# A hybrid decoder step on one core: conditioning vectors, result copies, query layout and a buffer moved together

## The chip, the cores and the metric

The kernel runs on 1 core of one Trainium2 chip. The metric is the device time of one execution of the whole program, in microseconds (us). One core has five engines with a queue of instructions each: TensorE (PE; its weight loads are shown as PEld), VectorE (DVE), ScalarE (ACT), GpSimd (POOL) and SyncE (SP), which here does nothing but issue transfers. Each engine takes its instructions in the order in which they stand in its queue, and an instruction that has to wait holds up the rest of the queue.

## The reference: what is computed

One layer of a decoder with two kinds of heads side by side, for a prompt of 1024 rows and for 8 samples of 4 rows (1056 rows in all), 1024 wide, in float32:

```python
sh1, sc1, g1, sh2, sc2, g2 = split(silu(c) @ w_ada + b_ada)      # conditioning: 9 vectors c, 6 parts of 1024
u = x * (1 + sc1) + sh1
mq, mk, mv, mo, mi, mf, nq, ck, cv, sk, sv, wk, wv, ng = split(u @ w_in)
h = mlstm(mq, mk, mv, mi, mf, mo)            # 4 heads of 128: a matrix memory in chunks
o = nsa(nq, ...)                             # 8 query heads of 64 in 2 groups: compressed, selected, window keys
x = LN(alpha * x + g1 * (concat(h, o) @ w_out))
u2 = x * (1 + sc2) + sh2
y = LN(alpha * x + g2 * (relu(u2 @ w_up) ** 2 @ w_down))
```

Returned beside y are the key and value rows of the step (ck, cv, sk, wk, sv, wv), the window cache moved on by four rows, and the states of the matrix memory. Only sh1 and sc1 (the first third of the conditioning) are needed for the input projection; g1 is needed after w_out, the rest from the feed-forward on.

## The kernel before

Rows are kept as columns: a tile is [128 features, rows]. Most products run as three products of two halves (a high and a low part, made by `split`: one ACT copy, one DVE subtraction). The order of the work:

- **Start.** `ada_part(G, c0, ...)` (L140) is one unit of the conditioning: four 512 KB pieces of w_ada (tile wada) are loaded over SP, 32 narrow products per unit are made (L147; the trace counts two instructions for each), then a copy and a transposition (L151) follow. There are 12 units: G is the third (0, 1, 2), c0 goes from 0 to 3. The four of G = 0 run here, with four wada buffers. Then come u and its split (uh, ul), the compression of the cache, and the products for v and the gates (L292).
- **Projections.** `proj` (L357) makes one 128-column tile of `u @ w_in` in three chunks of rows, 24 products each; its loop gives control back six times per chunk. `nsa_tile(mt)` (L454) projects one tile and stores it in DRAM: through a staging tile rw with three buffers into d_q (queries, tiles 16 to 19), d_k or d_ck. Tiles 14 to 19 come first, with the gate chain between them; then the attention of the samples (L785 to L891, its pool on the right side of memory and four banks of PSUM); then tiles 12 and 13, the compression for the prompt (`cmp_prompt`, L470), and the first steps of the matrix-memory heads (`run_dense(FILL)`).
- **Attention.** For each of 64 (group, block of 128 queries, head) `score_steps` (L959) makes scores, softmax and a probability tile P, of which there are NP = 4; `turn` (L1014) transposes it, `products` (L1059) multiplies with V. `attention_kv` (L919) and `attention_v` (L938) load keys and values once per group, `q_prep` (L946) loads queries once per block from d_q, all through the tag "qr", which has one buffer. Beside it run the "dense" steps: `mlstm_steps` (L540), with the eight remaining conditioning units in it (`ada_unit`, L530, wada with two buffers), and, when those are done, the output projection (`wout_steps`). A loop (L1175 to L1211) lays the three streams out by model costs: attention in all counts 196, dense DEN_TOTAL, and whichever is behind its share goes next.
- **End.** Output projection and first norm, the up projection in 16 pairs (`up_pair`, L1431: a Strassen-like scheme, weights aw with three buffers, results to d_r), the down projection (L1530) and the second norm.

Four copies of results from DRAM to DRAM are written at the head of attention (L913 to L917): o_v (1.1 MB), o_kT twice (1.1 MB each) and o_win (2.1 MB).

The text gives the order in which things are traced. The order in each engine's queue is set when the program is built, from a simulated timeline (`schedule_with_timeline_sim=True`): an instruction whose inputs are there can stand ahead of one written earlier. So the trace has the o_v copy at 94.94 us, in the middle of the projections, though it is written after them. A pool that is opened where another has been closed waits, tile by tile, until the old tiles have been read.

Of the kernel before, what the change touches and what calls it, by code (L numbers as in the profile page):

```python
# [31 lines left out]
T = 1056  # L32
# [26 lines left out]
def _body(tc, nc, top, io, dbg):  # L59
# [55 lines left out]

    d_q = mk(dr, [128, 4, T], F32, "d_q")
    d_k = mk(dr, [2, 128, T], F32, "d_k")
# [21 lines left out]

    def ada_part(G, c0, wpool, wbufs, pp, ps, ptile):  # L140

        for k in range(8):
            if k % 2 == 0:
                w = mk(wpool, [128, 2, 4, 128], F32, "wada", bufs=wbufs, name=f"wada{G}{c0}{k}")
                SP.dma_start(w, io["w_ada"][G, c0, :, k:k + 2])
            for j in range(4):
                PE.matmul(ps[32 * j:32 * j + 32, 0:128], lhsT=sil[:, k, :], rhs=w[:, k % 2, j],  # L147
                          start=(k == 0), stop=(k == 7), tile_position=(0, 32 * j))
        sb = mk(pp, [128, 128], F32, "adasb", bufs=1, name=f"adasb{G}{c0}")
        ACT.copy(sb, ps[:, 0:128])  # L150
        PE.transpose(ptile[:, 0:128], sb, ident)  # L151
        v = ptile[:, 0:128].rearrange("p (j i) -> p j i", j=4)
        DVE.tensor_tensor(out=adaT[:, 4 * G:4 * G + 4, c0], in0=v[:, :, 0:9],
                          in1=bc(badaT[:, 16 * G + c0:16 * G + 16:4], 9), op=ALU.add)

    sc1p = mk(ce, [128, 8, 9], F32, "sc1p")
# [296 lines left out]

    def nsa_tile(mt, between=None):  # L454
        def evac(ps, c, t0, n):
            rw = mk(pB, [128, 384], F32, "rw", bufs=3, name=f"rw{mt}_{c}")
            if mt >= 16:
                ACT.mul(rw[:, 0:n], ps[:, 0:n], -0.125)  # L458
                SP.dma_start(d_q[:, mt - 16, t0:t0 + n], rw[:, 0:n])
            else:  # L460
                ACT.copy(rw[:, 0:n], ps[:, 0:n])
                dst = (d_ck if mt < 14 else d_k)[mt % 2]
                SP.dma_start(dst[:, t0:t0 + n], rw[:, 0:n])
            next(between or iter(()), None)
        for _ in proj(mt, evac):
            pass

# [34 lines left out]

    gates = gate_chain()
    for mt in (14, 15, 16, 17, 18, 19):
        nsa_tile(mt, gates)
    for _ in gates:
        pass
    sA.close()
    if "stopB" in dbg:
# [4 lines left out]
    d_gt1 = d_gt.rearrange("a (h c) t -> a h (c t)", h=4)  # L514
    mps = {}

# [5 lines left out]

    LATP, DEN_TOTAL, FILL = 8.0, 240.0, 22.0

    ada_todo = [(1, 0), (1, 1), (1, 2), (1, 3), (2, 0), (2, 1), (2, 2), (2, 3)]
    pw_ada = {}

    WA, SL = 2, (0, 1)

    def ada_unit():  # L530
        if not ada_todo or "p" not in pw_ada:
            return
        G, c0 = ada_todo.pop(0)
        pa = mtile(f"ada{G}{c0}")
        pt = mtile(f"adat{G}{c0}")
        ada_part(G, c0, pw_ada["p"], WA, pm, pa, pt)

    heads_done = [False]

    def mlstm_steps():  # L540
        for h in range(4):
# [14 lines left out]
            yield 1.0, 2.5  # L556
            if ada_todo and 'p' in pw_ada:
                ada_unit()
                yield 1.9, 2.5
            kT = tile_A("b", f"kT{h}")  # L560
# [34 lines left out]
            yield 1.8, 2.5  # L595
            ada_unit()
            yield 1.9, 2.5
            qT = tile_A("a", f"qT{h}")
# [16 lines left out]
            for c0, nn in ((0, 3), (3, 3), (6, 2)):  # L615
# [15 lines left out]
                yield 1.2, 2.5  # L631
            if h in SL:
                ada_unit()
                yield 1.9, 2.5
            rstd_of(rs, mv[:, :, 1], EPS)
# [150 lines left out]
    for g in range(2):  # L786
        for e in range(2):
            SP.dma_start(qr[64 * g:64 * g + 64, e::2], d_q[64 * e:64 * e + 64, 2 * g:2 * g + 2, 1024:T])
    kn = mk(pS, [128, 2, 32], F32, "kn")
# [99 lines left out]
    for g in range(2):  # L889
        for e in range(2):  # L890
            SP.dma_start(d_mix[2][64 * e:64 * e + 64, 4 + 2 * g:6 + 2 * g, 256:288], mN[64 * g:64 * g + 64, e::2])  # L891
    nsa_tile(12)
    nsa_tile(13)
    cmp_prompt(0)
    cmp_prompt(1)
    run_dense(FILL)
    s2.close()
    sB.close()
# [5 lines left out]
    mps["p"] = psa  # L904
    pw_ada["p"] = pat
    WMX = mk(pat, [128, 384], F32, "WMX")
# [3 lines left out]
    POOL.memset(zer, 0.0)  # L910


    SP.dma_start(io["o_v"], d_v)  # L913
    for x, d in ((0, d_ck), (2, d_k)):
        SP.dma_start(io["o_kT"][x:x + 2].rearrange("j p t -> p j t"), d.rearrange("j p t -> p j t"))
    with after_last():
        SP.dma_start(io["o_win"].rearrange("b t c -> t b c"), io["win_raw"][:, 4:256, :].rearrange("b t c -> t b c"))  # L917

    def attention_kv(g):  # L919
        NT = mk(pat, [128, 4, 256], F32, "NT", bufs=1, name=f"NT{g}")  # L920

        SP.dma_start(NT, bass.AP(d_rt.tensor, d_rt.offset + 127 + 4 * g * 128 * 383, [[382, 128], [128 * 383, 4], [1, 256]]))
        CB = mk(pat, [128, 4, 120], F32, "CB", bufs=1, name=f"CB{g}")
        POOL.memset(CB[:, :, 0:47], 0.0)
        POOL.memset(CB[:, :, 63:120], BIG)
        POOL.tensor_copy(CB[:, :, 47:63], NT[:, :, 15:256:16])
        K = [mk(pat, [128, 1024], F32R, f"K{j}", bufs=1, name=f"K{g}{j}") for j in range(2)]
        for hb in range(2):
            for j in range(2):
                kr = mk(pat, [128, 512], F32, "qr", bufs=1, name=f"kr{g}{j}{hb}")  # L930
                for hf in range(2):
                    SP.dma_start(kr[64 * hf:64 * hf + 64], d_k[j, 64 * g:64 * g + 64, 512 * hb:512 * hb + 512])
                kk = K[j][:, 512 * hb:512 * hb + 512]
                ACT.copy(kk, kr)
                DVE.tensor_tensor(out=kk[64:128], in0=kr[64:128], in1=kk[64:128].bitcast(F32), op=ALU.subtract)
        return NT, CB, K

    def attention_v(g):  # L938
        V = mk(pat, [128, 2, 8, 128], F32R, "V", bufs=1, name=f"V{g}")
        for j in range(2):  # L940
            vr = mk(pat, [128, 8, 64], F32, "qr", bufs=1, name=f"vr{g}{j}")
            SP.dma_start(vr, d_v[0:1024, 128 * j + 64 * g:128 * j + 64 * g + 64].rearrange("(b p) d -> p b d", p=128))
            split(nc, V[:, j, :, 0:64], V[:, j, :, 64:128], vr)
        return V

    def q_prep(g, qb):  # L946
        t0 = 128 * qb
        q0 = mk(pat, [128, 4, 128], F32, "qr", bufs=1, name=f"qr{g}{qb}")
        for hf in range(2):
            for e in range(2):  # L950
                SP.dma_start(q0[64 * hf:64 * hf + 64, e::2], d_q[64 * e:64 * e + 64, 2 * g:2 * g + 2, t0:t0 + 128])
        QH = mk(pat, [128, 4, 128], F32R, "QH", bufs=2, name=f"QH{g}{qb}")
# [71 lines left out]

    NS, NP = 2, 4
    L_S, L_P, L_T = 1.6, LATP, 1.9
# [148 lines left out]
    while not (qs.end and qp.end and dn_end):  # L1175
# [23 lines left out]
        else:  # L1199
# [8 lines left out]
            else:  # L1208
                nxt = min(best, dn_at)
                assert nxt < 1e7  # L1210
                now[0] = max(t, nxt)  # L1211
    assert not ada_todo
    if not filled:
# [261 lines left out]
    for p in range(15):  # L1475
        up_pair(p)
        if p == 0:
            su.close()


# [351 lines left out]
```

## Time and profile before

| | |
|---|---|
| time, median of 3 runs | 1604.46 us (1595.38, 1604.53, 1604.46) |
| the profiled execution | 1598.26 us, of which the span on the core is 1596.5 us |
| PE busy | 1497.3 us (94%) |
| VectorE busy | 1074.8 us (67%) |
| ScalarE busy | 630.1 us (39%) |
| GpSimd busy | 306.0 us (19%) |
| mean granted clock of TensorE | 0.979 |
| moved by DMA | 204.11 MB, mean 128 GB/s |

By the trace the start takes until about 94 us, the projections until about 240, attention until about 770, the output projection and the norm until about 880, the up projection until about 1212, the down projection and the last norm the rest.

How to read it: a busy time is the union of an engine's instructions. The idle time before an instruction is put down to whoever released it ("<-"). The granted clock is the share of full speed at which TensorE was allowed to run. An engine that is idle matters only if it is the one that sets the end.

### The profile page before, as it was taken

The page shows a single profiled execution, that of the slowest core. Times are in us where ns is not written, and L with a number is a line of the kernel's source. Part 1 is how long each engine was busy: PE and PEld are TensorE (multiplying, and loading weights), DVE is VectorE, ACT ScalarE, POOL GpSimd, SP SyncE. Part 2 cuts the span into 40 slices and gives each one's busy share as a digit, 9 for nine tenths or more (in the row PEclk, how much of TensorE's full clock was granted, in tenths as well). Part 3 has the DMA queues.
Part 4 walks back from the last instruction along what each step waited for, and adds up shares of the span by engine and source line. Part 5 has one row for each costly group of instructions (what it writes and reads, how often), then busy time and mean ns, then how long its engine had stood idle before and what let it go on. Part 6 is the DMA issues. An engine that isn't in the chain of part 4 may idle for free.

```text
span 1596.5 us, 30052 instructions
## 1 busy us (share of the span) xinstructions
PE 1497.3 (94%) x11647; PEld 1434.2 (90%) x11647; DVE 1074.8 (67%) x2366; ACT 630.1 (39%) x1258; POOL 306.0 (19%) x383
## 2 busy tenths in 40 slices
PE   6899999899999899999998699999999999998976
PEld 5799899799999799889797699999999999998975
DVE  2521223666766476977577977776768788879888
ACT  2432233645555455655356422222226433232301
POOL 0000001433232233335102500000001111203244
PEclk9999999999999899999999799999999999999988
DMA  8756553342233421343564453333324342412222
GB/s 296 266 180 209 180 158 113 102 136 90 75 114 110 108 70 57 122 108 104 161 201 134 164 208 117 106 105 104 108 82 147 137 144 68 143 59 73 90 85 83
DMA packets 113337, 204.11 MB, mean 128 GB/s; under 512 B 18881, under 2 KB 63850, under 8 KB 112266
## 3 DMA queue, kind: packets, MB, share of 16 engines
q1 hardware_dynamic: 111898, 200.87, 39.2%
q8 instruction: 92, 1.51, 0.4%
q10 hardware_dynamic: 1296, 1.31, 0.2%
q14 instruction: 51, 0.42, 0.1%
HBM read 162.95 MB, written 46.07 MB: 131 GB/s over the span
## 4 chain that ended last, share of the span: by engine, by line
PE 69%; DVE 15%; DMA 8%; issue 2%; ACT 2%; SPq 2%; POOL 1%; DVEq 0%; ACTq 0%
PE p L1311 19%; PE pj L348 13%; PE pd L1537 11%; PE po L348 5%; PE o L1062 4%; PE S L981 3%; PE pt L1021 3%; DVE oplT L51 2%; DMA wada<-in_w_ada 2%; DVE ophT L51 2%; DVE A L1548 2%; PE pA L292 2%; DVE acc L1542 1%; PE ada L147 1%; DMA w<-in_cmp_w 1%
## 5 line engine op out<-in xcount | busy, mean ns | idle before, releaser
L1537 PE MATMUL pd<-oplT,ophT 128*128 128x264 f32 x2352 | 290.5, 286 | 8.5 <-DVE acc L1542 4.4
L1537 PEld LDWEIGHTS pd<-oplT,ophT 128*128 128x128 f32 x2352 | 289.5, 189 | 9.4 <-DVE ophT L51 4.7
L1004 POOL TENSOR_SCALAR P<-P,l,sg 128x64 f32<-128x64 f32 (+8 forms) x192 | 128.5, 682 | 215.7 <-DVE l L1001 207.8
L51 DVE TENSOR_TENSOR PTl<-pt,PTh 128x512 fp32r<-128x512 f32 (+1 forms) x160 | 102.0, 645 | 29.6 <-ACT PTh L50 28.7
L998 ACT ACTIVATE P<-P,mn 128x640 f32<-128x640 f32 (+7 forms) x128 | 94.2, 737 | 63.0 <-DVE mn L822 52.2
L50 ACT CAST PTh<-pt 128x512 fp32r<-128x512 f32 (+1 forms) x160 | 86.5, 549 | 79.3 <-PE pt L1021 77.2
L348 PE MATMUL pj<-uh,wt_h 128*128 128x384 f32 (+1 forms) x576 | 115.8, 330 | 2.1 <-ACT rw L458 2.1
L348 PE MATMUL pj<-uh,wt_l 128*128 128x384 f32 (+1 forms) x576 | 116.2, 330 | 0.0
L348 PE MATMUL pj<-ul,wt_h 128*128 128x384 f32 (+1 forms) x576 | 115.9, 330 | 0.0
L1548 POOL TENSOR_TENSOR A<-A,A 128x1024 f32<-128x1024 f32 x7 | 24.1, 3453 | 478.3 <-DVE ophT L51 478.3
L50 ACT CAST ophT<-A 128x1024 fp32r<-128x1024 f32 x49 | 51.3, 1050 | 138.0 <-PE pd L1537 90.2
L1021 PE MATMUL pt<-ident,P 128*128 128x128 f32 x592 | 97.3, 275 | 3.1 <-POOL P L1004 3.1
L348 PEld LDWEIGHTS pj<-uh,wt_h 128*128 128x128 f32 x576 | 93.9, 188 | 4.3 <-ACT rw L458 2.8
L348 PEld LDWEIGHTS pj<-uh,wt_l 128*128 128x128 f32 x576 | 95.0, 188 | 2.5 <-issue 1.8
L348 PEld LDWEIGHTS pj<-ul,wt_h 128*128 128x128 f32 x576 | 95.2, 190 | 0.8 <-issue 0.4
L1062 PE MATMUL o<-PTh,V 128*128 128x256 f32 x264 | 80.7, 312 | 1.2 <-ACT PTh L50 0.9
L1542 DVE TENSOR_TENSOR acc<-acc,pd 128x264 f32<-128x264 f32 (+1 forms) x126 | 61.8, 515 | 26.0 <-PE pd L1537 26.0
L1062 PE MATMUL o<-PTl,V 128*128 128x256 f32 x264 | 73.1, 297 | 3.6 <-DVE PTl L51 3.2
L1021 PEld LDWEIGHTS pt<-ident,P 128*128 128x128 f32 x592 | 70.2, 141 | 5.9 <-POOL P L1004 3.5
L981 PE MATMUL S<-K,QH 128*128 128x512 f32 (+3 forms) x200 | 71.7, 362 | 2.8 <-DVE mn L822 2.2
L51 DVE TENSOR_TENSOR oplT<-B,oplT 128x1056 fp32r<-128x1056 f32 x49 | 72.6, 1481 | 0.4 <-ACT oplT L50 0.2
L51 DVE TENSOR_TENSOR ophT<-A,ophT 128x1024 fp32r<-128x1024 f32 x49 | 66.1, 1351 | 9.5 <-ACT ophT L50 9.5
(1095 smaller groups left out, 3463.9 us busy)
## 6 DMA issues: line engine op xcount, KB each, us to landing
wada<-in_w_ada SPq DMA_DIRECT2D x48, 512.0 KB
aw<-in_w_up SPq DMA_DIRECT2D x32, 512.0 KB
d_r<-C SPq DMA_DIRECT2D x62, 264.0 KB
B<-d_r SPq DMA_DIRECT2D x28, 528.0 KB
A<-in_w_down SPq DMA_DIRECT2D x28, 512.0 KB
wst<-in_w_t SPq DMA_DIRECT2D x24, 512.0 KB
wst<-in_w_out SPq DMA_DIRECT2D x24, 512.0 KB
w<-in_cmp_w SPq DMA_DIRECT2D x4, 1024.0 KB
```

The costliest lines, as they stand in the source:

```text
L50: nc.scalar.copy(hi, src)
L51: nc.vector.tensor_tensor(out=lo, in0=src, in1=hi.bitcast(F32), op=ALU.subtract)
L348: PE.matmul(ps[:, 0:n], lhsT=a[:, k, :], rhs=b[:, k, t0:t0 + n], start=(i == 0 and k == 0), stop=(i == 2 and k == 7))
L981: PE.matmul(S[:, 0:w], lhsT=Q[:, r], rhs=K[j][:, k0 + c0:k0 + c0 + w], start=(i == 0), stop=(i == 1))
L998: ACT.activation(P[:, o:o + n], P[:, o:o + n], AF.Exp, bias=mn[:, br:br + 1], scale=-1.0, accum_out=l[:, br:br + 1])
L1004: POOL.tensor_scalar(P[:, a:b], P[:, a:b], l[:, x:x + 1], sg[:, qb, y:y + 1], op0=ALU.mult, op1=ALU.mult)
L1021: PE.transpose(pt[:, 256 * x + 128 * e:256 * x + 128 * e + 128], P[:, o:o + 128], ident)
L1062: PE.matmul(op, lhsT=vv, rhs=ps[e][:, 256 * x:256 * x + 256], start=(x0 + x == 0 and e == 0), stop=(x0 + x == len(bl) - 1 and e == 1))
L1311: PE.matmul(ps[:, 0:HH], lhsT=w[a][:, k], rhs=ops[name][b][:, k, HH * h:HH * h + HH], start=(i == 0 and k == 0), stop=(i == 2 and k == 3))
L1537: PE.matmul(ps[h][:, 0:HH], lhsT=x[:, 128 * m:128 * m + 128], rhs=y[:, HH * h:HH * h + HH], start=(i == 0), stop=(i == len(mms) - 1))
L1542: DVE.tensor_tensor(out=out, in0=out, in1=x, op=ALU.add)
L1548: eng.tensor_tensor(out=r[out], in0=r[a], in1=r[b], op=op)
```

## The change

- The conditioning units of G = 1 and 2 leave `mlstm_steps`. `ada_part` becomes a generator, `ada_steps`, that stops once in the middle of a unit. `ada_rest(G, ...)` goes through the four units of a third, with a pool of its own (four wada buffers, two banks of PSUM). `nsa_tile` takes it as `more` and moves it on three times per tile: G = 1 beside tiles 14 to 19, G = 2 beside tiles 12 and 13 and the compression, with what is left in front of attention. For G = 2 the pool of the sample attention is closed before tile 12 instead of before attention.
- The four result copies move into the up projection, one behind each of pairs 1 to 4, on SP after that pair's last transfer.
- d_q is laid out as [64, 8, T], by head. A projected tile is stored by two transfers of 64 partitions instead of one of 128; the queries of a block are loaded by two transfers instead of four.
- The tag "qr" has two buffers instead of one, P has five instead of four. DEN_TOTAL goes from 240 to 223, FILL from 22 to 18.

```diff
-    d_q = mk(dr, [128, 4, T], F32, "d_q")
+    d_q = mk(dr, [64, 8, T], F32, "d_q")
...
-    def ada_part(G, c0, wpool, wbufs, pp, ps, ptile):
+    def ada_steps(G, c0, wpool, wbufs, pp, ps, ptile):
         for k in range(8):
+            if k == 4:
+                yield
...
-    def nsa_tile(mt, between=None):
+    def nsa_tile(mt, between=None, more=None):
         def evac(ps, c, t0, n):
...
-                SP.dma_start(d_q[:, mt - 16, t0:t0 + n], rw[:, 0:n])
+                for e in range(2):
+                    SP.dma_start(d_q[:, 2 * (mt - 16) + e, t0:t0 + n], rw[64 * e:64 * e + 64, 0:n])
...
-        for _ in proj(mt, evac):
-            pass
+        for i, _ in enumerate(proj(mt, evac)):
+            if i % 6 == 3:
+                next(more or iter(()), None)
...
+    def ada_rest(G, stack):
+        pD = pool(f"pD{G}", stack, side="right")
+        psD = pool(f"psD{G}", stack, space=PSUM)
+        mps["p"] = psD
+        for c0 in range(4):
+            pa = mk(psD, [128, 512], F32, "ada", bufs=1, name=f"ada{G}{c0}")
+            pt = mk(psD, [128, 512], F32, "adat", bufs=1, name=f"adat{G}{c0}")
+            yield from ada_steps(G, c0, pD, 4, pD, pa, pt)
+            yield
...
-    gates = gate_chain()
+    gates, rest = gate_chain(), ada_rest(1, sD)
     for mt in (14, 15, 16, 17, 18, 19):
-        nsa_tile(mt, gates)
+        nsa_tile(mt, gates, rest)
     for _ in gates:
         pass
+    for _ in rest:
+        pass
+    sD.close()
...
-    LATP, DEN_TOTAL, FILL = 8.0, 240.0, 22.0
+    LATP, DEN_TOTAL, FILL = 8.0, 223.0, 18.0
...
-            ada_unit()                       # three places in mlstm_steps
-            yield 1.9, 2.5
...
-    nsa_tile(12)
-    nsa_tile(13)
+    s2.close()
+    sD = ExitStack()
+    rest = ada_rest(2, sD)
+    nsa_tile(12, None, rest)
+    nsa_tile(13, None, rest)
     cmp_prompt(0)
+    next(rest, None)
     cmp_prompt(1)
+    for _ in rest:
+        run_dense(4.0)
     run_dense(FILL)
-    s2.close()
+    sD.close()
...
-    SP.dma_start(io["o_v"], d_v)             # and o_kT twice, o_win
...
-                kr = mk(pat, [128, 512], F32, "qr", bufs=1, name=f"kr{g}{j}{hb}")
+                kr = mk(pat, [128, 512], F32, "qr", bufs=2, name=f"kr{g}{j}{hb}")
...
-            for e in range(2):
-                SP.dma_start(q0[64 * hf:64 * hf + 64, e::2], d_q[64 * e:64 * e + 64, 2 * g:2 * g + 2, t0:t0 + 128])
+            SP.dma_start(q0[64 * hf:64 * hf + 64], d_q[:, 4 * g:4 * g + 4, t0:t0 + 128])
...
-    NS, NP = 2, 4
+    NS, NP = 2, 5
...
         up_pair(p)
...
+        if 0 < p < 5:
+            with after_last():
+                if p < 3:
+                    SP.dma_start(io["o_kT"][2 * p - 2:2 * p].rearrange("j p t -> p j t"), (d_ck, d_k)[p - 1].rearrange("j p t -> p j t"))
+                elif p == 3:
+                    SP.dma_start(io["o_v"], d_v)
+                else:
+                    SP.dma_start(io["o_win"].rearrange("b t c -> t b c"), io["win_raw"][:, 4:256, :].rearrange("b t c -> t b c"))
```

More of the change, by code (lines that the diff above doesn't have):

```diff
@@ L154, in ada_part @@
                           in1=bc(badaT[:, 16 * G + c0:16 * G + 16:4], 9), op=ALU.add)
+    def ada_part(*a):
+        for _ in ada_steps(*a):
+            pass
     sc1p = mk(ce, [128, 8, 9], F32, "sc1p")
@@ L501, in cmp_prompt @@
             split(nc, vcP[:, :, 0:64], vcP[:, :, 64:128], vc)
-    gates = gate_chain()
+    def ada_rest(G, stack):
[7 more added lines that the diff above has]
+            yield
+    mps = {}
+    sD = ExitStack()
+    gates, rest = gate_chain(), ada_rest(1, sD)
     for mt in (14, 15, 16, 17, 18, 19):
-        nsa_tile(mt, gates)
+        nsa_tile(mt, gates, rest)
     for _ in gates:
         pass
+    for _ in rest:
+        pass
+    sD.close()
     sA.close()
@@ L514, in _body @@
     d_gt1 = d_gt.rearrange("a (h c) t -> a h (c t)", h=4)
-    mps = {}
     def mtile(name):
@@ L521, in tile_A @@
         return mk(pm, [128, T], F32, tag, bufs=1, name=name)
-    LATP, DEN_TOTAL, FILL = 8.0, 240.0, 22.0
[L525 to L536, printed above, removed]
+    LATP, DEN_TOTAL, FILL = 8.0, 223.0, 18.0
     heads_done = [False]
@@ L556, in mlstm_steps @@
             yield 1.0, 2.5
-            if ada_todo and 'p' in pw_ada:
-                ada_unit()
-                yield 1.9, 2.5
             kT = tile_A("b", f"kT{h}")
@@ L595, in mlstm_steps @@
             yield 1.8, 2.5
-            ada_unit()
-            yield 1.9, 2.5
             qT = tile_A("a", f"qT{h}")
@@ L631, in mlstm_steps @@
                 yield 1.2, 2.5
-            if h in SL:
-                ada_unit()
-                yield 1.9, 2.5
             rstd_of(rs, mv[:, :, 1], EPS)
@@ L786, in _body @@
     for g in range(2):
-        for e in range(2):
-            SP.dma_start(qr[64 * g:64 * g + 64, e::2], d_q[64 * e:64 * e + 64, 2 * g:2 * g + 2, 1024:T])
+        SP.dma_start(qr[64 * g:64 * g + 64], d_q[:, 4 * g:4 * g + 4, 1024:T])
     kn = mk(pS, [128, 2, 32], F32, "kn")
@@ L891, in _body @@
             SP.dma_start(d_mix[2][64 * e:64 * e + 64, 4 + 2 * g:6 + 2 * g, 256:288], mN[64 * g:64 * g + 64, e::2])
-    nsa_tile(12)
-    nsa_tile(13)
+    s2.close()
+    sD = ExitStack()
+    rest = ada_rest(2, sD)
+    nsa_tile(12, None, rest)
+    nsa_tile(13, None, rest)
     cmp_prompt(0)
+    next(rest, None)
     cmp_prompt(1)
+    for _ in rest:
+        run_dense(4.0)
     run_dense(FILL)
-    s2.close()
+    sD.close()
     sB.close()
@@ L904, in _body @@
     mps["p"] = psa
-    pw_ada["p"] = pat
     WMX = mk(pat, [128, 384], F32, "WMX")
@@ L910, in _body @@
     POOL.memset(zer, 0.0)
-    SP.dma_start(io["o_v"], d_v)
[L914 to L917, printed above, removed]
     def attention_kv(g):
@@ L940, in attention_v @@
         for j in range(2):
-            vr = mk(pat, [128, 8, 64], F32, "qr", bufs=1, name=f"vr{g}{j}")
+            vr = mk(pat, [128, 8, 64], F32, "qr", bufs=2, name=f"vr{g}{j}")
             SP.dma_start(vr, d_v[0:1024, 128 * j + 64 * g:128 * j + 64 * g + 64].rearrange("(b p) d -> p b d", p=128))
@@ L947, in q_prep @@
         t0 = 128 * qb
-        q0 = mk(pat, [128, 4, 128], F32, "qr", bufs=1, name=f"qr{g}{qb}")
+        q0 = mk(pat, [128, 4, 128], F32, "qr", bufs=2, name=f"qr{g}{qb}")
         for hf in range(2):
-            for e in range(2):
-                SP.dma_start(q0[64 * hf:64 * hf + 64, e::2], d_q[64 * e:64 * e + 64, 2 * g:2 * g + 2, t0:t0 + 128])
+            SP.dma_start(q0[64 * hf:64 * hf + 64], d_q[:, 4 * g:4 * g + 4, t0:t0 + 128])
         QH = mk(pat, [128, 4, 128], F32R, "QH", bufs=2, name=f"QH{g}{qb}")
@@ L1211, in _body @@
                 now[0] = max(t, nxt)
-    assert not ada_todo
     if not filled:
```

## The prediction

> **What bounds the kernel now.** I read the page first, then the engines' busy time in stretches of 20 us, then who PE (the matrix engine) waited for, and last single stretches of the timeline where it waited.
>
> ```profile
> span 1596.5 us, 30052 instructions
> PE 1497.3 (94%) x11647; PEld 1434.2 (90%) x11647; DVE 1074.8 (67%) x2366; ACT 630.1 (39%) x1258; POOL 306.0 (19%) x383
> ...
> 100.00:120.00 20.00, 20.00 (x126) 18.83 (x125) 5.03 (x20) 6.23 (x11) 0.00 (x0) 1.00 0.84 243
> 160.00:180.00 20.00, 18.18 (x115) 16.88 (x115) 3.28 (x9) 2.92 (x5) 0.00 (x0) 1.00 0.50 176
> 220.00:240.00 20.00, 20.00 (x176) 19.00 (x175) 4.37 (x9) 5.62 (x16) 0.00 (x0) 1.00 0.24 90
> 280.00:300.00 20.00, 14.23 (x131) 12.40 (x131) 9.94 (x45) 10.42 (x39) 7.66 (x20) 0.95 0.41 120
> 520.00:540.00 20.00, 16.68 (x143) 15.82 (x141) 11.91 (x46) 9.82 (x34) 5.85 (x19) 1.00 0.39 97
> 540.00:560.00 20.00, 15.51 (x115) 14.22 (x116) 7.97 (x36) 9.11 (x29) 4.39 (x9) 0.74 0.41 111
> 640.00:700.00 60.00, 55.10 (x392) 48.97 (x390) 57.27 (x197) 40.65 (x95) 26.98 (x41) 1.00 0.41 111
> ```
>
> The columns are the stretch, its length, busy PE, weight loads, VectorE (DVE), ScalarE (ACT), GpSimd (POOL), granted clock, DMA share, GB/s. PE works 1497 of 1596 us, so only its idle time and its slow clock are to be had: an instruction taken from one PE-full stretch and put into another is worth nothing. The projections (94 to 240) are PE-full; in attention (240 to 700) three stretches stand out, and the end of it is VectorE's (57.27 of 60).
>
> ```profile
> PE ada L147 <- DMA wada<-in_w_ada: 9.2, 4, 3.9
> PE pt L1021 <- POOL P L1004: 3.1, 2, 2.8
> ...
> PE S L981 <- ACT QH L50: 0.4, 1, 0.4
> ...
> PE ada L147 <- DVE Cs L592: 0.8, 2, 0.6
> ...
> PE pj L348 <- ACT rw L458: 2.1, 2, 1.8
> ...
> SPq L145 <- PE ada L147: 42.7, 17, 16.3
> ```
>
> These are waits: total, times, longest. The first four are PE's from 240 to 700, the fifth is its only wait from 92 to 240, the last is the SP queue's from 240 to 700. The largest is the conditioning step itself: its weight pieces (wada, two buffers) arrive late. The last row tells why others suffer too: SP stood 42.7 us before a wada transfer whose buffer was still being read, and whatever stood behind it on SP stood as well. One such place:
>
> ```profile
> 534.20 1.08 PE L147 MATMUL ada<-wada,sil 128*32 128x128 f32 x32 [0.22 <-DVE Cs L592]
> 540.54 1.08 PE L147 MATMUL ada<-wada,sil 128*32 128x128 f32 x16 [3.65 <-DMA wada<-in_w_ada]
> 552.95 0.55 PE L1021 MATMUL pt<-ident,P 128*128 128x128 f32 x3 [2.84 <-POOL P L1004]
> ...
> 536.00 0.59 SPq L145 DMA_DIRECT2D wada<-in_w_ada  x1
> 536.64 1.95 SPq L951 DMA_DIRECT2D qr<-d_q  x3
> ...
> 294.00:298.00 4.00, 0.39 (x3) 0.18 (x2) 1.58 (x8) 2.50 (x11) 1.46 (x3) 1.00 0.79 226
> 298.00:302.00 4.00, 3.70 (x32) 3.02 (x32) 1.50 (x7) 1.50 (x3) 0.82 (x1) 0.57 0.49 166
> 540.00:544.00 4.00, 2.37 (x33) 1.40 (x34) 0.23 (x1) 0.85 (x2) 0.00 (x0) 0.57 0.90 235
> 544.00:548.00 4.00, 4.00 (x21) 3.86 (x21) 2.40 (x10) 1.45 (x7) 0.50 (x1) 0.58 0.67 211
> 552.00:556.00 4.00, 3.05 (x18) 3.05 (x18) 2.45 (x10) 2.68 (x10) 1.66 (x4) 0.77 0.28 66
> 556.00:560.00 4.00, 4.00 (x30) 4.00 (x30) 1.20 (x9) 2.21 (x5) 1.27 (x3) 0.80 0.00 0
> ```
>
> Queries for the next block (qr) go out only after the wada transfer. And each long wait of PE is followed by a stretch at 0.57 of the clock.
>
> **The change, part by part.** The sum is made against the profiled execution, 1598.26 us.
>
> *Conditioning out of attention.* Gone are PE's waits for wada, 9.2, and the 0.8 before the step: **-10.0**. What would PE have waited for otherwise? The queries at 543, but those were late because they stood behind wada. Gone with the waits is the slow clock behind them, busy time times the missing clock: 3.70 x 0.43 + 2.37 x 0.43 + 4.00 x 0.42 = 1.6 + 1.0 + 1.7 = **-4.3**. The Trainium skill (TensorE: Matmul & The Clock Gate, What's actually happening) says that about one idle window of 3.4 us halves the matrix clock; the waits of 3.65 and 3.91 with 0.57 behind them agree. By that rule new waits under 3.4 us cost no clock, as the 2.84 us wait, with 0.77 behind it, rather contradicts.
>
> *The matrix work itself* is moved, not removed:
>
> ```profile
> L147 PE MATMUL ada<-wada,sil 128*32 128x128 f32 x512 | 21.3, 291 | 10.0 <-DMA wada<-in_w_ada 9.2 <-DVE Cs L592 0.8
> ```
>
> Eight units, 21.3 us, leave attention and enter the projections, where PE has no idle time except the 2.1 us named below. **0** net.
>
> *Its transfers in the projections.* 32 loads of 512 KB, 16.8 MB in all, in two bursts: four units beside tiles 14 to 16, four beside tiles 12 and 13 and the compression. PE waits in order, so a late load stops all projection work behind it. Nearest rows:
>
> ```profile
> PE ada L147 <- DMA wada<-in_w_ada: 12.3, 9, 3.9
> ...
> 20.00:56.00 36.00, 32.63 (x319) 26.69 (x317) 11.87 (x21) 12.65 (x24) 0.00 (x0) 1.00 0.96 336
> 92.00:140.00 48.00, 48.00 (x294) 45.49 (x293) 10.85 (x36) 15.39 (x33) 0.19 (x1) 1.00 0.66 200
> 140.00:170.00 30.00, 27.88 (x174) 26.99 (x172) 2.88 (x4) 6.54 (x11) 0.00 (x0) 1.00 0.77 252
> 205.00:240.00 35.00, 35.00 (x312) 32.94 (x311) 10.24 (x35) 11.46 (x32) 0.13 (x1) 1.00 0.43 139
> ```
>
> Over the whole span these waits are 12.3 us in 9, so the first group's four units, run with four buffers while the DMA engines were at 0.96, waited 12.3 - 9.2 = 3.1 us in 5. The new groups have four buffers too. Twice 3.1 is 6.2 where DMA is full; the projections have 200 and 139 GB/s against 336 there, and lose the result copies. I take **+5**, by that row; the ends are 0 and what attention paid, 10.0 + 4.3 = 14.3. Queued behind a wada transfer on SP there: the projection's weights, its result stores (three rw buffers) and the sample branch's loads.
>
> *Result copies.* Today they run inside the projections:
>
> ```profile
> 153.55 0.92 SPq L917 DMA_DIRECT2D o_win<-in_win_raw  x1
> 154.57 6.21 SPq L459 DMA_DIRECT2D d_q<-rw  x3
> ...
> L459 SPq DMA_DIRECT2D d_q<-rw x12: 319/374/5233, 128.7 to 170.2; - x12
> ...
> 154.57 11.02 DMA d_q<-rw
> ```
>
> Behind the 2 MB o_win copy the issue of one store took 5.2 us instead of 0.37 and its landing 11.02, and the rw buffers ran out: that is PE's 2.1 us. Gone: **-2.1**. In the up projection each copy goes behind a pair's last store on SP; behind it stand stores of later products and weights (aw) of the pair after next. PE is full there, at DMA shares that leave room, and already meets such bursts:
>
> ```profile
> 906.00:926.00 20.00, 20.00 (x154) 20.00 (x154) 17.91 (x34) 4.35 (x7) 0.00 (x0) 0.92 0.76 265
> ...
> 909.18 1.66 SPq L1488 DMA_DIRECT2D A<-in_w_down  x3
> ...
> DVE s L1445 <- DMA aw<-in_w_up: 13.3, 13, 3.1
> ```
>
> 2 MB of w_down pieces at 908 left PE at 20.00 of 20. But VectorE waits for aw 13 times already, so the slack is about a microsecond. I take **+1**, by the w_down burst; ends 0 and SP's hold behind o_win, 0.92 + 5.2 = 6.1.
>
> *Queries by head.* Stores become two of 64 partitions: 12 more issues at 0.37 us, 4.4 us of SP beside full PE work. Loads need two issues instead of four:
>
> ```profile
> L951 SPq DMA_DIRECT2D qr<-d_q x64: 573/601/1640, 262.4 to 648.7; - x64
> ```
>
> 32 fewer at 0.6 us, 1.2 us earlier for each block's queries; with two staging buffers a load need not wait for the split before it. This shortens the chain that ended in 0.4 and 2.84 us of PE wait and 3.05 x 0.23 + 4.00 x 0.20 = 1.5 us of clock, 4.7 together. I take **-3**; ends 0 and -4.7. The Trainium skill (DMA: Bandwidth & Descriptors, Rules for kernel authors) advises one 128-partition transfer over two to disjoint halves, since these share the engines; that speaks against the stores, and by it their sum would be the 4.4 us of SP and no gain.
>
> *Fifth probability buffer, FILL 18, DEN_TOTAL 223.* They shift which fill stands where; nothing in the waits names a probability buffer as missing. **0**, ends -3 and +3, the 3.1 us for P above.
>
> Sum: -10.0 - 4.3 + 5 - 2.1 + 1 - 3 = **-13.4**: 1584.9. With all ends one way: 1598.26 - 24.1 = 1574 and 1598.26 + 9.1 = 1607 (the 2.1 then not gained). The runs shown (1595.38, 1604.53, 1604.46) stand 3 below to 6 above the profiled one; I put the forecast 2 above the sum: **1587**.
>
> **Rivals.** (a) *The wait is moved, not removed* (25%): the loads stall PE in the projections as they did in attention, +14.3 instead of +5, or SP's hold before wada starves the rw stores. For it: 252 GB/s before any of it is added in 140 to 170. Against: four buffers, and the 4.2 MB of copies that leave. 1587 + 9 = 1596, with the copies at their end 1601.
>
> (b) *Slower: attention starts late* (7%). The second group's 8.4 MB can come in only after the sample branch's tiles are released (its buffers lie there, behind s2.close), and attention's pools only open after it. At 252 GB/s that is 33 us. It decides when less other PE work than this stands planned there; then PE sits it out: 1587 + 33 = 1620. Against: compression and head 0's steps filled PE at 35.00 of 35.
>
> (c) *More than the waits* (18%): with SP free of its 42.7 us, key, value and query loads all come earlier, PE's small waits in 640 to 700 shrink and the new loads cost nothing: the lower end, 1574.
>
> (d) *The waits stay under another name* (5%): SP's holds belong to the query chain itself, and PE waits for QH where it waited for wada: -10.0 and -4.3 fall away, 1601.
>
> **How the numbers follow.** Forecast 45%, its own range 1578 to 1595. A measurement here tells about 1% from no change, so faster means below 1588.4: 0.6 of the forecast and all of (c), 0.45. Slower is (b), 0.07. The rest, 0.48, is the same. The range takes (a), half of (c) and (d): 1572 to 1602; left out are (b), the lower half of (c) and a little of each side, under 0.2.
>
> **What would show it.** Right: no wait for wada after about 265 us; no granted clock under 0.9 from 280 to 600; no wait of PE for rw; under 6 us of PE waits for wada from 92 to 265; PE full from 906 to 1200. Wrong: PE waits for wada or rw over 10 us in the projections (a); a first score product later than the moved 21 us explain, with PE idle before it (b); PE idle behind QH at the second key group (d); or waits for aw on PE in the up projection.

## The result, and the profile after

The changed kernel took 1575.61 us (median of 4 runs, 1570.15 to 1580.96) against 1604.49 us before (4 runs): a ratio of 0.983, 95% interval [0.981, 0.985]. It is faster by 1.7%, inside the range and 11 us below the forecast of 1587. The profiled execution took 1580.96 us with a span of 1579.2; against the profiled execution of before (1598.26, span 1596.5) it is 17.3 us shorter, where the sum had said 13.4. The medians lie further apart, 28.9 us, since the profiled execution of before was one of its faster ones and that of the changed kernel its slowest; the stages below account for the 17.3 only.

The head of the page, then PE's waits of the changed kernel from 92 to 300 us and from 300 to 700 us (total, times, longest). The conditioning step is L149 now, the load of its weights L147:

```profile
span 1579.2 us, 30041 instructions
PE 1494.8 (95%) x11647; PEld 1436.4 (91%) x11647; DVE 1072.5 (68%) x2366; ACT 629.0 (40%) x1258; POOL 308.6 (20%) x383
...
PE ada L149 <- DMA wada<-in_w_ada: 6.4, 5, 2.6
PE pj L354 <- ACT rw L468: 1.1, 1, 1.1
...
PE po L354 <- ACT m0mh L50: 2.7, 1, 2.7
PE o L1060 <- DVE PTl L51: 2.6, 2, 1.7
PE pt L1019 <- POOL P L1002: 1.0, 1, 1.0
```

In attention no wait for wada is left, nor any for a query (QH). Into the projections came 6.4 us for wada, and of the 2.1 us for rw half stayed. The busy times of single stretches (stretch, length, PE, weight loads, DVE, ACT, POOL, clock, DMA share, GB/s):

```profile
280.00:300.00 20.00, 20.00 (x142) 19.55 (x140) 7.31 (x12) 5.84 (x11) 3.97 (x3) 1.00 0.35 104
...
640.00:700.00 60.00, 55.56 (x422) 48.57 (x422) 46.75 (x159) 34.13 (x77) 27.83 (x36) 0.97 0.28 71
906.00:1000.00 94.00, 94.00 (x770) 94.00 (x770) 71.78 (x131) 21.59 (x37) 0.00 (x0) 1.00 0.61 201
1000.00:1100.00 100.00, 100.00 (x820) 100.00 (x819) 71.21 (x125) 24.12 (x42) 0.00 (x0) 1.00 0.31 106
1100.00:1190.00 90.00, 90.00 (x738) 90.00 (x738) 63.17 (x110) 24.73 (x39) 0.00 (x0) 1.00 0.25 85
```

The 14.23 of 20 from 280 to 300 is 20.00 now, because the last conditioning units stand there in front of attention. VectorE's crowded stretch, 57.27 of 60 before, is at 46.75. From 906 to 1190, where the copies run, PE is full, so they cost it no idle time.

Fixed stretches compare badly here, since 21.3 us of matrix work changed its stage. So I cut both spans at events: the first projection work, the first score product S, the last product o, the first product of the up projection. Before, then after, one row for each of projections, attention, and the tail between attention and up projection:

```profile
92.60:267.70 175.10, 172.98 (x1165) 162.99 (x1165) 41.06 (x119) 49.36 (x106) 5.54 (x15) 1.00 0.59 181
267.70:789.00 521.30, 497.48 (x3860) 465.16 (x3859) 354.50 (x1168) 281.51 (x700) 171.72 (x289) 0.98 0.34 102
789.00:884.10 95.10, 82.16 (x559) 74.53 (x557) 73.73 (x173) 54.93 (x94) 15.16 (x20) 0.97 0.55 172
```

```profile
92.50:302.40 209.90, 202.34 (x1727) 183.63 (x1726) 44.39 (x131) 52.14 (x116) 6.53 (x16) 0.98 0.65 203
302.40:783.40 481.00, 470.85 (x3335) 447.46 (x3336) 355.28 (x1162) 279.12 (x691) 172.53 (x288) 0.99 0.27 79
783.40:862.10 78.70, 72.55 (x521) 69.55 (x519) 66.23 (x159) 51.80 (x89) 14.28 (x20) 0.98 0.57 180
```

Length less PE's busy time is PE's idle time: 2.1, 23.8 and 12.9 before, 7.6, 10.2 and 6.2 after. The second loss is clock: busy time times the clock that was missing, which I summed over stretches of 4 us, because the rows above round the clock too coarsely. It was 0.0, 8.5 and 0.1 before, 3.1, 3.1 and 1.5 after. Together: **projections +8.6, attention -19.0, tail -5.3**; the same sums give +2.1 in the up projection, +1.9 in the down projection, and -0.3 before 92 us. That is 12 of the 17.3; the other 5 lie inside time that counts as busy, and I can't place them.

### The profile page after: what moved, and what is told of

The parts are those of the page before. It is cut to its first block, busy times and chain, and to the rows that moved or that the text cites. A ratio compares the mean times of both kernels' runs of the same rounds, so it can differ in the third digit from the quotient of the medians.

```text
span 1579.2 us, 30041 instructions
## 1 busy us (share of the span) xinstructions
PE 1494.8 (95%) x11647; PEld 1436.4 (91%) x11647; DVE 1072.5 (68%) x2366; ACT 629.0 (40%) x1258; POOL 308.6 (20%) x383
## 4 chain that ended last, share of the span: by engine, by line
PE 76%; DVE 13%; DMA 5%; issue 3%; ACT 2%; SPq 1%; POOL 0%; DVEq 0%; ACTq 0%
PE p L1308 19%; PE pj L354 16%; PE pd L1543 11%; PE po L354 6%; PE o L1060 4%; PE pt L1019 4%; PE S L979 4%; DMA wada<-in_w_ada 2%; DVE oplT L51 2%; DVE ophT L51 2%; PE pA L298 2%; PE hidS L277 2%; DVE A L1554 2%; DVE acc L1548 1%; PE ada L149 1%
## 5 line engine op out<-in xcount | busy, mean ns | idle before, releaser
L354 PE MATMUL pj<-uh,wt_l 128*128 128x384 f32 (+1 forms) x576 | 120.3, 333 | 0.0
L979 PE MATMUL S<-K,QH 128*128 128x512 f32 (+3 forms) x200 | 71.6, 362 | 0.9 <-DVE mn L823 0.7
```

The costliest lines, as they stand in the source:

```text
L354: PE.matmul(ps[:, 0:n], lhsT=a[:, k, :], rhs=b[:, k, t0:t0 + n], start=(i == 0 and k == 0), stop=(i == 2 and k == 7))
L979: PE.matmul(S[:, 0:w], lhsT=Q[:, r], rhs=K[j][:, k0 + c0:k0 + c0 + w], start=(i == 0), stop=(i == 1))
```

## The experiments

There were three series, each on a chip of its own; every kernel is compared with before on the same chip, and series are compared by ratio. The changed kernel ran with the result and in series 1 only; its two ratios, 0.983 and 0.987, lie some 5 us apart, and a distance "from the changed kernel" is given from both. The table gives, for each kernel, idle time plus clock loss of PE in the three stages, cut and summed as above, PE's busy time in the tail, and the ratio. The short names stand in the headings below.

| kernel | projections | attention | tail | PE busy in tail | ratio to before, 95% |
|---|---|---|---|---|---|
| before | 2.1 + 0.0 | 23.8 + 8.5 | 12.9 + 0.1 | 82.2 | 1 |
| changed | 7.6 + 3.1 | 10.2 + 3.1 | 6.2 + 1.5 | 72.6 | 0.983 [0.981, 0.985] |
| changed again (e4) | 6.9 + 1.6 | 7.5 + 3.3 | 6.6 + 1.6 | 73.1 | 0.987 [0.984, 0.989] |
| conditioning only (e1) | 11.3 + 4.3 | 14.3 + 0.0 | 17.7 + 1.6 | 59.7 | 1.003 [1.001, 1.004] |
| copies only (e2) | 0.0 + 0.0 | 21.8 + 11.9 | 12.9 + 1.9 | 83.9 | 0.999 [0.997, 1.001] |
| queries by head only (e3) | 2.1 + 0.0 | 17.6 + 4.4 | 15.1 + 1.4 | 88.0 | 0.993 [0.990, 0.996] |
| without copies (f1) | 11.4 + 5.5 | 9.2 + 0.0 | 15.5 + 1.6 | 76.0 | 0.994 [0.992, 0.996] |
| without queries (f2) | 7.8 + 2.9 | 8.7 + 5.1 | 14.9 + 2.4 | 58.7 | 0.996 [0.994, 0.998] |
| four P buffers (f3) | 7.6 + 4.5 | 9.7 + 5.0 | 11.5 + 4.4 | 60.5 | 0.993 [0.991, 0.995] |
| later start (f4) | 5.8 + 1.4 | 7.2 + 4.8 | 7.1 + 0.0 | 71.6 | 0.983 [0.981, 0.985] |
| five P buffers, plan of four (g1) | 6.4 + 1.5 | 10.9 + 3.4 | 17.1 + 3.5 | 59.8 | 0.993 [0.991, 0.996] |
| pace of before (g2) | 6.9 + 4.6 | 6.6 + 0.0 | 14.4 + 3.3 | 59.1 | 0.989 [0.987, 0.991] |
| one staging buffer (g3) | 9.2 + 2.8 | 11.4 + 8.9 | 17.7 + 2.0 | 59.0 | 0.998 [0.996, 0.999] |
| pace 228 (g4) | 7.6 + 1.4 | 9.6 + 5.1 | 11.4 + 1.6 | 66.1 | 0.989 [0.987, 0.992] |

One caution first. The builder orders each engine's queue anew from its simulated timeline, so an edit moves more than it names. I compared the sequence of PE's operations in the traces, consecutive ones on the same tiles taken together: copies only has exactly the sequence of before, later start agrees with the changed kernel in 99%. Of every other variant only 44 to 71% agrees with the kernel that it was made from.

### Series 1: each part alone

**Conditioning only (e1)**: before, with the conditioning units moved and the pacing constants of the change.

```diff
+    gates, rest = gate_chain(), ada_rest(1, sD)
     for mt in (14, 15, 16, 17, 18, 19):
-        nsa_tile(mt, gates)
+        nsa_tile(mt, gates, rest)
...
-    LATP, DEN_TOTAL, FILL = 8.0, 240.0, 22.0
+    LATP, DEN_TOTAL, FILL = 8.0, 223.0, 18.0
```

> The kernel before with the conditioning units moved out of attention (four wada buffers, FILL 18, DEN_TOTAL 223), copies, query layout and buffers as before. The sum of the prediction has -10.0 - 4.3 + 5 = -9.3 us for this part: about 1595 against 1604.5. Rival 'buffers': the wait is only moved, and what pays is the memory that the move frees (a second query buffer, a fifth P): 1600 to 1606. Rival 'queue': SP freed of its 42.7 us before wada pulls every attention load forward: 1580 or less, nearly the whole gain.

Measured: 1603.75 us against 1601.21, no gain but a loss of 0.3%. The stages tell where: attention gets what the prediction promised and more (idle and clock 32.3 before, 14.3 here), the projections give 13.5 back, and the tail 6.3. In the projections the loads meet the result copies. SP's timeline (start, duration, issue), then PE's waits from 170 to 240 us and one stretch of all engines:

```profile
132.75 0.94 SPq L923 DMA_DIRECT2D o_win<-in_win_raw  x1
133.80 8.73 SPq L147 DMA_DIRECT2D wada<-in_w_ada  x1
142.63 0.37 SPq L465 DMA_DIRECT2D d_q<-rw  x1
...
PE pj L354 <- ACT wt_h L50: 4.4, 1, 4.4
PE SS L831 <- DVE mnS L823: 2.3, 1, 2.3
...
140.00:170.00 30.00, 30.00 (x248) 28.82 (x247) 4.40 (x9) 8.46 (x20) 0.19 (x1) 1.00 0.73 254
```

The issue of one wada load behind the o_win copy holds SP for 8.73 us, where the median of all 48 is 0.36. That this hold causes PE's waits is not shown. PE is full during it and behind it, until 195 us (the row shows 140 to 170). The two waits end at 198 us (2.3) and at 214 us (4.4), more than 50 us after the hold. And the next weights, for whose split (wt_h) PE waits the 4.4 us, are issued at 207.38, behind the last cache load of the sample branch; in the changed kernel they are issued at 191.81, in the midst of these loads. So the order of SP's queue differs there as well, and it is the nearer cause of the 4.4 us.

**Copies only (e2)**: the copies taken out of the projections and put behind pairs 1 to 4 of the up projection, nothing else.

> The kernel before with the four result copies moved into the up projection, nothing else. Sum of the prediction: -2.1 + 1 = -1.1 us, no difference that can be seen, and no wait of PE for rw in the projections. Rival 'copies': they cost attention and projections more than the rw wait shows: 1590 to 1597.

Measured: 1598.99 us, no difference that can be told. With PE's sequence unchanged this is the cleanest of the runs. PE's wait for rw is gone (the row of all engines from 92 to 240 us):

```profile
92.00:240.00 148.00, 148.00 (x1010) 139.38 (x1009) 33.16 (x107) 41.32 (x91) 1.67 (x11) 1.00 0.53 155
```

PE is full for all 148 us. The 2.1 us that this is worth do not show in the time; in this profile attention's clock loss is higher by more than that, 11.9 against 8.5.

**Queries by head only (e3)**: before with the new layout of d_q, two load issues for a block instead of four, still one staging buffer.

```diff
-    d_q = mk(dr, [128, 4, T], F32, "d_q")
+    d_q = mk(dr, [64, 8, T], F32, "d_q")
...
         for hf in range(2):
-            for e in range(2):
-                SP.dma_start(q0[64 * hf:64 * hf + 64, e::2], d_q[64 * e:64 * e + 64, 2 * g:2 * g + 2, t0:t0 + 128])
+            SP.dma_start(q0[64 * hf:64 * hf + 64], d_q[:, 4 * g:4 * g + 4, t0:t0 + 128])
```

> The kernel before with d_q laid out by head (stores in two halves, loads in two transfers instead of four), still one buffer for the queries, nothing else. Sum of the prediction: at most the -3 us of the query chain, more likely half of it without the second buffer: 1602 to 1604. Rival 'layout': SP's issue time in attention was what held the loads: 1596 or less. Rival: the 12 more stores starve rw: 1606 or more, with PE waiting for rw over 4 us.

Measured: 1588.67 us, 0.993 [0.990, 0.996]: 11.5 us, four times the -3 of the prediction. The query loads' group, the waits for wada on PE from 240 to 700, and two stretches which the prediction showed for before:

```profile
L950 SPq DMA_DIRECT2D qr<-d_q x32: 573/608/775, 260.2 to 625.0; - x32
...
PE ada L147 <- DMA wada<-in_w_ada: 5.7, 6, 1.7
...
280.00:300.00 20.00, 17.62 (x172) 15.91 (x171) 11.54 (x53) 11.85 (x43) 9.54 (x20) 1.00 0.55 161
540.00:560.00 20.00, 18.93 (x170) 18.17 (x171) 16.69 (x70) 14.03 (x41) 9.72 (x20) 1.00 0.39 110
```

There are 32 issues for 64, as worked out. But what they buy is not query time: the waits *for wada* fall from 9.2 us (longest 3.9) to 5.7 (longest 1.7), and the clock in the two stretches from 0.95 and 0.74 to 1.00. PE has 3.4 us more busy time in each of the two stretches, and the clock that came back is worth 0.05 x 14.2 + 0.26 x 15.5 = 4.7 more: 11.5 in all, the size of the gain. That the two agree is partly chance: by the table, attention as a stage gained 10.3 us and the tail lost 3.5. So with this edit, conditioning still in attention, a part of the wait is gone that the conditioning move takes away, and the two terms may overlap. That fewer issues on SP do it is argued, not shown: PE's order changed with it, and SP's hold before wada fell only from 42.7 to 37.3 us.

**The changed kernel again (e4)**, beside these on the same chip:

> The changed kernel once more, to have its clock and span beside those of the parts on the same chip. If executions differ only by the granted clock, span times clock is the same in all of them within 0.1%, about 1543.5 us as in the four runs before (1544.5, 1543.7, 1542.5, 1543.2); if not, it scatters as the spans do, 0.7%.

Measured: 1578.04 us, 0.987. Span times clock spreads by 0.28% (1542.6 to 1546.9), the spans by 0.46%: the clock explains a part of the scatter, not all but 0.1% as expected. The parts alone make 1.003, 0.999 and 0.993, together -9 us; the whole makes -21 to -27. The three parts do not add up. The second staging buffer and the fifth P buffer, which use memory that the conditioning move frees, were not tried alone.

### Series 2: one part taken out of the changed kernel

**Without the copies' move (f1)**: the copies stand beside the projections again.

> The changed kernel with its result copies put back beside the projections, where before had them; all else as changed. Reference points: the changed kernel 1578.0 us, the copies moved alone -2.2 us against before. Theory of company (the copies hurt only since the conditioning loads share the projections' SP queue with them): PE waits for wada or for the wt split in the projections grow by 5 to 10 us, half-rate stretches appear behind them, the projections end some 14 us later (near 271 instead of 257) and the time is 10 to 14 us above the changed kernel, 1588 to 1592. Theory of the sum (each part is worth what it gave alone): 2 us above, 1580.

Measured: 1591.31 us, 0.994. In the projections the loss is as the theory of company has it, 16.9 instead of 8.5 to 10.7, and its rows are those of conditioning only; here too the weights that PE waits for are issued behind the last cache load (at 211.66):

```profile
135.59 0.97 SPq L923 DMA_DIRECT2D o_win<-in_win_raw  x1
137.42 7.15 SPq L147 DMA_DIRECT2D wada<-in_w_ada  x1
...
PE pj L354 <- ACT wt_h L50: 3.5, 1, 3.5
PE SS L831 <- DVE mnS L823: 2.3, 1, 2.3
```

Some 9 us more are in the tail, where no copy runs in either kernel: its idle time and clock loss are 17.1 instead of 7.7 to 8.2. So part of this difference is order, in the tail and, by SP's queue, perhaps in the projections too.

**Without the query edits (f2)**: old layout, one staging buffer.

> The changed kernel with the queries stored as before (four loads for each block of queries) and one staging buffer; all else as changed. Theory of overlap (stored by head alone gained 11.5 to 12.5 us because it shortened the same wada waits and half-rate stretches in attention that the conditioning move removes; once the wada loads are gone, SP has room for four loads): 0 to 4 us above the changed kernel, 1578 to 1582, no half-rate stretch from 300 to 600. Theory of the sum: the 12 us are SP's time for the query chain itself and are lost here: 1590, with PE waits for QH or the query loads late behind the splits. The prediction's term: +3, 1581.

Measured: 1594.34 us, 0.996. The time is that of the sum, but not for its reason. The theory of overlap was right that SP has no trouble: no wada wait comes back, and attention's idle time is 8.7. What is lost stands at its start and behind it. The first score product comes at 310.7 instead of 300.6 to 302.4. Most of that is work that has changed its place: PE is busy for 210.5 us before it instead of 201.1 to 202.3. But it waits 2.7 us for its query, with a stretch at 0.65 of the clock right behind (PE's waits):

```profile
PE S L980 <- ACT QH L50: 2.7, 1, 2.7
...
PE pn L1246 <- ACT xna L1268: 6.7, 1, 6.7
```

And the tail has only 58.7 us of matrix work instead of 73, with a wait of 6.7 us for the normalized rows (xna) in it.

**Four probability buffers (f3)**: `NS, NP = 2, 4`.

> The changed kernel with four probability buffers instead of five; all else as changed. The prediction's term is 0 (within 3): 1575 to 1581. Theory of the chain (the fifth buffer lets scores and softmax of a further block run ahead, so that PE's attention stretch has fewer waits behind P, PTl and mn): 3 to 8 us above, 1581 to 1586, with more PE wait behind P and PTl from 300 to 700 and last o later than 780.

Measured: 1591.39 us, 0.993, 10 to 16 us above the changed kernel where the prediction had 0. Waits behind PTl (the low half of the transposed probabilities) and mn (the row minimum that the softmax takes from the negated scores) grew by 1.8 us only (4.0 and 1.1 against 2.6 and 0.7); the tail again holds 60.5 us of matrix work and a wait for xna, 4.2 us.

**Later start (f4)**: `nsa_tile(mt, gates, rest if mt > 14 else None)`. In the changed kernel the first moved unit waits, and the clock goes. PE's timeline (start, duration, instruction, idle time before it and its releaser), and two stretches there:

```profile
108.88 1.08 PE L149 MATMUL ada<-wada,sil 128*32 128x128 f32 x16 [2.61 <-DMA wada<-in_w_ada]
...
108.00:112.00 4.00, 3.12 (x35) 2.01 (x36) 0.00 (x0) 1.04 (x1) 0.00 (x0) 0.53 1.08 442
112.00:116.00 4.00, 4.00 (x31) 3.20 (x31) 1.99 (x8) 0.40 (x1) 0.00 (x0) 0.62 0.96 403
```

> The changed kernel with the first group's conditioning loads begun beside projection tile 15 instead of tile 14; all else as changed. In the changed kernel the first of these units waits 2.6 us for wada at 109 and the clock is halved from 108 to 115, which costs some 3 us more. Theory that the wait is one of crowding at the start (the loads stand behind the weights and rope tables that are due at that moment): both go, 5 to 6 us less, 1572 to 1573, PE full and the clock at 1.00 from 92 to 140. Rival, that the wait moves along with the loads (any tile's weights crowd them): 1577 to 1579 and a wait of 2 to 4 us for wada near 125.

Measured: 1575.59 us, 0.983 [0.981, 0.985]. The wait and the slow clock are gone from there:

```profile
108.00:112.00 4.00, 4.00 (x50) 3.24 (x49) 1.71 (x8) 0.00 (x0) 0.00 (x0) 1.00 1.07 437
112.00:116.00 4.00, 4.00 (x25) 3.73 (x24) 0.90 (x5) 2.59 (x5) 0.00 (x0) 1.00 0.98 415
```

The projections' loss falls from 8.5 to 10.7 to 7.2; of the 5 to 6 us expected, a single profile shows 1.3 to 3.5. The time can't be told from the changed kernel's: the intervals overlap with both of its measurements. It is the best version that was run, by less than can be measured.

### Series 3: is it the part, or the order that comes with it?

Every kernel of series 2 but the later start had lost in the tail. So these four change the order with as little else as possible.

**Five buffers, plan of four (g1)**: the five buffers stay, but the planner lets scores run only four heads ahead.

```diff
-                    return self.at if v < done_heads[0] + NP else 1e8
+                    return self.at if v < done_heads[0] + 4 else 1e8
```

> The changed kernel with its five probability buffers, but written out by the planner's rule for four (a head's scores may start only four heads ahead of the products). It stands between the changed kernel (0.987 of before) and four buffers (0.993). Theory of order: the fifth buffer's 8 to 10 us come from the order of PE's work that the plan gives, above all how much of the output projection is left for the end of attention, and the room alone gives nothing: 0.993 of before (some 1590 us), a wait of 4 us or more for xna behind the last products, last o near 804. Theory of room: the buffer lets scores run ahead whatever the plan: 0.987 (1578), last o near 780.

Measured: 1590.50 us, 0.993, the same as four buffers. So the room alone gave nothing here, and a rule of the planner that moves only the written order costs 11 to 16 us, as much as taking the buffer away. That order is the whole of the buffer's worth is the likely reading; it isn't proved by two kernels whose sequences agree with each other in only 63%. The tail, and the wait in it:

```profile
797.90:874.80 76.90, 59.79 (x432) 55.87 (x430) 64.46 (x157) 48.05 (x86) 16.48 (x21) 0.92 0.47 152
...
PE pn L1245 <- ACT xna L1267: 6.8, 1, 6.8
```

**Pace of before (g2)**: DEN_TOTAL 240, FILL 22. **Pace 228 (g4)**: DEN_TOTAL 228 instead of 223.

> The changed kernel with the two pacing constants of before (DEN_TOTAL 240 and FILL 22 instead of 223 and 18), all else as changed. Theory of order (the ends of the gain depend on which fill is left for the tail, and the constants are set for one work list): 4 to 10 us above the changed kernel, 1582 to 1588, with PE's waits behind last o grown; the waits for wada in the projections unchanged at 5 to 6.4 us. Theory that the gain is in the waits removed only: 1578 within 3, since no load and no wait is changed.

> The changed kernel with DEN_TOTAL 228 instead of 223: a change of the pace by 2% that moves no load, buffer or layout, made only to see how far a mere shift of the written order moves the time. Theory that differences of 8 to 14 us between the versions are the worth of their parts: within 2 us of the changed kernel, 1576 to 1580. Theory that a good share of them is the order that each version happens to get: 4 us or more away from it, to either side, with the difference in PE's waits from 300 to 890 and none in the projections.

Measured: 1583.20 and 1583.78 us, both 0.989, where the changed kernel had 0.983 and 0.987. Their intervals reach into that of its second measurement, not of its first. No load, buffer or layout is changed, the waits for wada are the same (6.7 and 6.0), attention as a stage is as good or nearly (6.6 and 14.7 against 10.8 to 13.3), and the tail loses 17.7 and 13.0 instead of 7.7 to 8.2 (the rows are those of pace 228):

```profile
788.60:866.10 77.50, 66.10 (x477) 61.71 (x475) 63.63 (x155) 49.75 (x87) 15.03 (x20) 0.97 0.52 164
...
PE pn L1245 <- ACT xna L1267: 3.9, 1, 3.9
```

So constants that move nothing but the written order cost about 4 to 9 us by these ratios; the lower end is within what the measurement leaves open.

**One staging buffer (g3)**: queries by head, but one buffer for queries, keys and values.

> The changed kernel with one staging buffer for queries, keys and values instead of two, and the queries still stored by head. With old layout and one buffer it was 0.9961 of before, with both changed 0.987. Theory that the buffer does it (the load of a block's queries waits for the split of the block before): 0.994 to 0.996, 1591 to 1594, a PE wait behind QH of 2 us or more and first S near 310. Theory that the layout does it: 0.987, 1578 to 1580.

Measured: 1597.50 us, 0.998: 18 to 23 us above the changed kernel, as bad as undoing both query edits or worse. With conditioning out of attention the layout, which gave 11.5 us alone, gives nothing without the second buffer. ScalarE's casts to QH waited 23.5 us for query loads here and 17.0 in without queries, against 3.5 in the changed kernel. Whether the second buffer would do as much with the old layout was not run. The first score product comes at 312.8, 10 to 12 us later than in the changed kernel, with 7 to 8 us more of PE's work before it and a wait for its query:

```profile
312.75 0.44 PE L979 MATMUL S<-K,QH 128*128 128x128 f32 x2 [2.04 <-ACT QH L50]
...
PE S L979 <- DVE mn L823: 4.9, 6, 2.0
```

Here attention loses 20.3 as a stage, the worst of the kernels that have no conditioning in it, and the tail 19.7.

## Why the prediction was right, and where it was not

**What bounds it, and the direction: right.** PE's idle time and its slow clock were what could be had, and the conditioning waits in attention were the largest of it. Conditioning only and the changed kernel both show the -10.0 and -4.3 gone from attention: no wait for wada, and a clock loss of 8.5 that falls to 0.0 and 3.1.

**New waits in the projections, +5: about right, its clock left out.** 6.4 us in 5; under 6 from 92 to 265 held (5.1). Two signs missed by little: the last wait for wada came at 279 and not before 265, and 1.1 us for rw stayed. A wait of 2.61 us went with a clock of 0.53 to 0.62 from 108 to 116, 3.1 us more. So the projections lost 8.6 us, where +5 and -2.1 make 2.9. The Trainium skill (TensorE: Matmul & The Clock Gate, What's actually happening) puts the drop behind about one idle window of 3.4 us, and by that rule no such cost was due; here it came after less. So it did a second time in the changed kernel, at 316 us, and a third time at 664 (0.57, behind a wait of 2.7 us):

```profile
312.00:316.00 4.00, 2.84 (x20) 2.27 (x20) 1.87 (x17) 2.60 (x12) 1.50 (x5) 1.00 0.26 66
316.00:320.00 4.00, 4.00 (x23) 4.00 (x23) 3.48 (x19) 3.45 (x16) 2.13 (x4) 0.57 0.06 17
```

Of the 4 us before the drop only 1.16 were idle. The measurement decides: shorter waits can cost clock too. They need not: from 252 to 256 PE was busy for 1.99 of 4 us and the clock stayed at 1.00, so what decides is open. The stretch at 316 is the one under 0.9 from 280 to 600, where the prediction wanted none.

**Rival (a) came true only where the copies stay.** The projections lose 13.5 us more than before with conditioning only (it said +14.3), 14.8 in without copies, and 6.4 to 8.6 in the changed kernel. That its price fits is partly luck: of the 11.3 us idle with conditioning only just 3.4 are waits for wada, the rest is for the next weights and the sample branch. Alone the conditioning move, -9.3 by its three terms, is worth nothing: the ratio is 1.003. And the copies' term, -2.1 + 1, was right alone (no difference measured) and too small in company, where their move goes with 6 to 8 us in the projections, by SP's hold or by the order of its queue. The prediction had both rows, SP's 5.2 us behind o_win and the loads' place on SP, and set "the 4.2 MB of copies that leave" against (a); it did not price this as what the copies' move is worth.

**Queries by head, -3 with ends 0 and -4.7: mis-sized.** Alone the layout gave 11.5 us; taking both query edits out of the changed kernel costs 15 to 21. The step that failed is the bound: it counted only waits that bore the query's name and the slow clock behind them, and with the layout the waits for wada fell too. How much of the 11.5 is the layout's and how much the new order's stays open. From the Trainium skill's advice (DMA: Bandwidth & Descriptors, Rules for kernel authors) against two transfers to disjoint halves the prediction drew a case of no gain; the edit as a whole measured 0.993. That doesn't speak against the advice: the stores, to which it was applied, got dearer, 24 issues at a median of 0.58 us for 12 at 0.37. Within the change the layout without the second staging buffer gave nothing (g3).

**Fifth P buffer and pace, 0 within 3: wrong, as large a miss as the queries.** 10 to 16 us for the buffer, about 4 to 9 for the pace. "Nothing in the waits names a probability buffer as missing" was true, and is still: the room alone gave nothing (g1). The fifth buffer lets the planner write another order, in which more of the output projection is left behind the last product of attention. The prediction summed attention and stopped there; the tail, 5.3 us of the gain, is in none of its terms.

**The sum.** -13.4 was made of terms that hold alone, and missed in both directions: the ones above may overlap (queries with conditioning), go together (copies with loads, layout with the second buffer), or work through the order. The measured 1575.6 lies below the forecast's own range of 1578 to 1595; that it lies within the whole range owes something to luck, since several terms missed by about 10 us and not all to the same side. It came near (c)'s 1574, but not by (c): the new loads are not free, and PE's idle time from 640 to 700 hardly shrank, 4.9 to 4.4 us.

What stays open: how much of each variant's loss in the tail belongs to its edit and how much to the order that the builder happened to find. In seven variants the tail holds 66.1 us of matrix work or less, and each waits 3.9 to 7.1 us for xna; the changed kernel, its repeat and the later start hold 71.6 to 73.1, have no such wait, and lose 6.2 to 7.1 us idle. More work there is no cure by itself: before, copies only, queries by head only and without copies hold 76.0 to 88.0 and idle 12.9 to 15.5.

## What to carry to other kernels

Before an edit is priced at nothing because no wait names it, ask whether it changes the order in which work is written: here a rule of the planner that moves no load, buffer or layout cost 11 to 16 us, as much as the largest term of the sum, and a 2% change of a pacing constant some 4 to 9. Price parts of a change together where they share a queue: moving the copies alone gave no time that could be measured, and beside the conditioning loads it went with 6 to 8 us in the projections. And count the stage behind the one that is tuned: what the fill no longer covers is lost there.

## What the hardware showed that I had not expected

The issue of a load on SP took 7.15 to 8.73 us right behind the o_win copy, against a median of 0.36. In the up projection the same copy holds nothing. Its issue, the next one, and the group of the weight loads of that stage (count, then the shortest, median and longest issue in ns):

```profile
970.58 0.94 SPq L1484 DMA_DIRECT2D o_win<-in_win_raw  x1
975.41 0.34 SPq L1412 DMA_DIRECT2D d_r<-C  x1
...
L1431 SPq DMA_DIRECT2D aw<-in_w_up x32: 332/333/452, 863.2 to 1148.0; - x32
```

The next store was issued 3.9 us after the end of the copy's issue and took 0.34, and no weight load of the stage took over 0.45. In the projections the load came 0.1 to 0.9 us behind the copy. Whether the distance or the lighter traffic decides was not tried.

The spread of one kernel's runs is partly clock: the repeat of the changed kernel took 1574.3 us at a mean granted clock of 0.981 and 1581.7 at 0.978, and span multiplied by clock spreads by 0.3% over its six runs, the spans by 0.5%. It isn't the whole of it: in the 23 runs of before on the same chip the product spreads no less than the spans, 0.8 against 0.7%. A few microseconds between single profiles of two kernels can't be read as a difference, even with their clocks.
